# One-hot product and its transposes at a pair's beginning, norm parameters and last norm's rows ahead of the loop of rounds, router subtractions on VectorE

## The chip, the core and the metric

The kernel runs on one core of a Trainium2 chip. The metric is the device time of one execution in microseconds (us). In the profile PE is TensorE's matmuls, PEld its weight loads, DVE is VectorE, ACT is ScalarE, POOL is GpSimd and SP is SyncE, which issues most of the DMAs. L1612 is line 1612 of the kernel before; in the kernel after the same statements stand some lines lower.

## The reference, cut to what matters

Two blocks run one after the other on 256 tokens of width 1024. The first, two hybrid layers, takes the time to about 838 us and is not touched. The second has two layers; each is a mixer (three kinds of attention behind one input projection, and an output projection), a layer norm, a router and a mixture of experts (MoE), and a second layer norm.

```python
def second_block(...):
    h = layer_norm(x, ln_in_g, ln_in_b)
    for l in range(DEPTH):                                    # 2
        mix = mixer_sublayer(h, ...)
        h = layer_norm(DEEPNORM_ALPHA * h + mix, ln1_g[l], ln1_b[l])
        ffn = grouped_moe(h, router_w, router_bias, exp_w_gate[l], exp_w_up[l], exp_w_down[l])
        h = layer_norm(DEEPNORM_ALPHA * h + ffn, ln2_g[l], ln2_b[l])
    return h

def grouped_moe(h, ...):                                      # 16 experts in 4 groups, 2 per token
    scores = sigmoid(h @ router_w)
    ...                                                       # best group, two best experts in it
    dense_gates = ...                                         # gate of each token and expert, mostly 0
    for e in range(N_EXPERTS):
        a = silu(h @ w_gate[e]) * (h @ w_up[e])               # 1024 -> 512
        y = y + dense_gates[:, e:e + 1] * (a @ w_down[e])     # 512 -> 1024
    return y
```

Everything is float32.

## The kernel before

**The stages.** In the second block, layer 0's mixer runs from about 840 to 984 us, its router to 996, its MoE to 1220; then come a branch, a norm and layer 1's mixer to 1366, its router to 1378, its MoE to 1603, and the last norm with the output.

**The MoE.** Experts work on slots: each has 64 slots per round, to which its tokens are gathered by a matmul with a one-hot matrix `oh` (L1546, L1562). A round has all experts; further rounds, in the loop `tc.For_i(1, rounds)` (L1716), are for experts with more than 64 tokens, and with these data the loop's body is passed over. Its branch stops all engines at a barrier. Experts go in eight pairs. `pair` computes the gate projection `pg` and the up projection `pu` (two calls of `proj`, 8 steps of the contraction each, L1597), the activation `a` on VectorE (L1633, L1634), its four transposes on TensorE (L1638), the copy `aT` on ScalarE (L1640), and the down projection from `wd` (L1597 again). The results are scaled by the slot's gate and split in a high and a low part (L1671 on ScalarE, L1672 on VectorE). `combine` brings them back to token order by matmuls with `got` (L1655) and adds them to the state (L1657). `combine` is a generator of two steps, which runs in the next pair: `pump()` calls one step behind the up projection and one behind the copy `aT`.

`combine_T` makes `got` and the slots' gates `gs`: a product of one-hot and gate on VectorE (`go`, L1607), two transposes (L1612), and two VectorE operations on them (L1615, L1616). In pairs 0 to 6 it is called behind the copy `aT`, in front of the down projection. The last pair differs (`done` is set): it calls `combine_T` ahead of the gate projection, pumps the pair before's combine between gate and up, and splits the down projection in four quarters of 256 columns. Within a quarter, behind the first of four steps (`mid` at k == 1), it combines the quarter before and takes its statistics for the norm (L802).

**Weights.** SP issues the transfers in the order of the code, into a ring of 1 MB places; a pair needs 12 of them (4 gate, 4 up, 4 down). A place is filled again when TensorE has read it. Behind the last pair SP issues the first pieces of the next mixer's input projection `w_in`.

**Router.** VectorE ranks the scores in small operations (L1506 to L1530), TensorE turns the mask `mb` into positions, and VectorE makes the one-hot. ScalarE meanwhile normalises the state and copies it to `hn[0]`; `hn[1]` is the rest, by subtraction: columns 0 to 511 on POOL (L1502), the others on VectorE (L1569).

**Norm and mixer's start.** Behind the branch, `norm_params` (L810 to L817) takes mean, reciprocal deviation and their product from the statistics; `normalise` (L826, L827) applies them; 16 transposes (L855) with copies in high and low parts (L1207 to L1210) lead to the first gemm, whose weights are split in two parts by ScalarE (L278) and VectorE (L279). The last norm brings its gain and shift rows to all partitions by four matmuls (L833); VectorE's six operations (L1758, L1759) read them from PSUM, POOL's two (L1750, L1751) from copies in SBUF.

## Time and profile before

| | us |
|---|---|
| median of 3 runs | 1619.72 (1618.51 to 1620.62) |
| the profiled execution | 1618.68 |
| its span in the trace | 1616.4 |
| PE busy in the span | 1510.0 (93%) |
| DVE / ACT / POOL busy | 976.5 / 736.3 / 251.8 |
| bytes moved by DMA | 419.71 MB, mean 260 GB/s |

The span is what the trace covers; 2.3 us of the execution lie around it. A row of a timeline has the start of a group of like instructions, the group's length, engine, line, operation, what is written and read, the count (xN), and in brackets how long the engine had been idle and what ended that. One 512-wide float32 matmul of the program stands there as two records. The page says that TensorE is busy nearly all the time, but the mean hides stages with different limits: in the MoE stages the transfers are saturated as well, and around the branch and in the tail nearly everything waits for short chains on VectorE and ScalarE. Stages have to be read apart.

### The profile page before, as it was taken

How to read it: one execution, taken by the hardware profiler on the slowest of the kernel's cores; microseconds unless marked ns; L12 is line 12 of the kernel's file. 1: busy time of each engine (PE TensorE's matmuls, PEld its weight loads, DVE VectorE, ACT ScalarE, POOL GpSimd, SP SyncE). 2: the span in 40 equal slices, each digit the busy share in tenths (PEclk: the TensorE clock that was granted, in tenths of full speed). 3: DMA queues.
4: the chain of work that ended last, by engine and by line, in shares of the span. 5: the costliest groups of instructions: out<-in, count | busy, mean ns of one | idle time of the engine just before them, and what ended most of it. 6: DMA issues, size and time to landing. Idle time of an engine off the chain costs nothing. (4 is left out here: it accounts for less than half of the span.)

```text
span 1616.4 us, 24413 instructions
## 1 busy us (share of the span) xinstructions
PE 1510.0 (93%) x9211; PEld 1092.7 (68%) x9211; DVE 976.5 (60%) x1894; ACT 736.3 (46%) x1403; POOL 251.8 (16%) x279
## 2 busy tenths in 40 slices
PE   6999999999999999999989998999988998999996
PEld 5877888888887888888878775334437776344332
DVE  4869777777786767777557774322137767222224
ACT  3466645655456664556446664112115565111112
POOL 0334640001242363000003100000001210000000
PEclk9999999999999999999999998999998999999998
DMA  9766769557854675965526368999985558899992
GB/s 346 245 215 236 261 219 353 181 179 235 313 186 136 218 271 185 318 207 174 164 73 209 128 222 300 403 407 407 407 314 168 179 180 315 314 407 406 407 405 92
DMA packets 278476, 419.71 MB, mean 260 GB/s; under 512 B 12722, under 2 KB 147748, under 8 KB 278348
## 3 DMA queue, kind: packets, MB, share of 16 engines
q1 hardware_dynamic: 273052, 398.63, 69.5%
q0 software_dynamic: 5152, 19.14, 3.4%
q8 instruction: 77, 1.26, 0.3%
q14 instruction: 51, 0.42, 0.1%
q10 hardware_dynamic: 144, 0.26, 0.0%
HBM read 416.94 MB, written 1.05 MB: 259 GB/s over the span
## 5 line engine op out<-in xcount | busy, mean ns | idle before, releaser
L279 DVE TENSOR_TENSOR split<-raw,split 128x1024 fp32r<-128x1024 f32 (+4 forms) x330 | 411.7, 1251 | 114.3 <-ACT split L278 111.2
L289 PE MATMUL mm<-hl,split 128*128 128x512 f32 x1168 | 412.6, 397 | 0.0
L278 ACT CAST split<-raw 128x1024 fp32r<-128x1024 f32 (+4 forms) x330 | 328.7, 1000 | 131.6 <-PE mm L323 69.5
L290 PE MATMUL mm<-hl,split 128*128 128x256 f32 x1168 | 326.3, 279 | 1.0 <-DVE split L279 1.0
L289 PEld LDWEIGHTS mm<-hl,split 128*128 128x128 f32 x1168 | 219.0, 187 | 50.4 <-issue 0.7
L1597 PE MATMUL mm<-raw,xg 128*64 128x512 f32 x1024 | 230.9, 602 | 1.1 <-ACT xg L1564 1.1
L290 PEld LDWEIGHTS mm<-hl,split 128*128 128x128 f32 x1168 | 220.3, 189 | 1.5 <-DVE split L279 1.3
L1597 PEld LDWEIGHTS mm<-raw,xg 128*64 128x64 f32 x1024 | 71.5, 138 | 136.5 <-issue 118.7
L289 PE MATMUL mm<-ahl,split 128*128 128x512 f32 x352 | 123.4, 395 | 0.0
L306 ACT COPY t<-mm 128x256 f32<-128x256 f32 x152 | 56.4, 371 | 142.7 <-PE mm L290 133.7
L1597 PE MATMUL mm<-raw,t 128*64 128x512 f32 (+1 forms) x576 | 114.8, 549 | 1.4 <-ACT t L1640 1.4
L321 PE MATMUL mm<-split,hl 128*128 128x512 f32 (+4 forms) x272 | 102.3, 376 | 4.2 <-ACT split L278 3.2
L290 PE MATMUL mm<-ahl,split 128*128 128x256 f32 x352 | 98.3, 279 | 0.3 <-DVE split L279 0.3
L322 PE MATMUL mm<-split,hl 128*128 128x512 f32 (+4 forms) x272 | 96.4, 355 | 1.0 <-DVE split L279 1.0
L323 PE MATMUL mm<-split,hl 128*128 128x512 f32 (+4 forms) x272 | 96.4, 355 | 0.3 <-POOL hl L1210 0.2
L306 DVE TENSOR_TENSOR t<-mm,t 128x256 f32<-128x256 f32 x140 | 59.1, 422 | 47.9 <-ACT t L306 47.7
L1633 DVE SCALAR_TENSOR_TENSOR t<-t,mm 128x512 f32<-128x512 f32 x16 | 11.0, 686 | 123.3 <-ACT t L1632 123.3
L1597 PEld LDWEIGHTS mm<-raw,t 128*64 128x64 f32 x576 | 39.4, 137 | 63.8 <-issue 53.4
L1672 DVE SCALAR_TENSOR_TENSOR t<-mm,s,t 128x512 fp32r<-128x512 f32 (+1 forms) x36 | 24.9, 692 | 94.9 <-ACT t L1671 94.9
L1671 ACT ACTIVATE t<-mm,s 128x512 fp32r<-128x512 f32 (+1 forms) x36 | 23.0, 640 | 129.9 <-PE mm L1597 129.9
L289 PEld LDWEIGHTS mm<-ahl,split 128*128 128x128 f32 x352 | 66.0, 187 | 15.5 <-ACT t L1095 0.2
L1640 ACT COPY t<-at 128x512 f32<-128x512 f32 x16 | 9.4, 586 | 129.7 <-PE at L1638 129.7
(426 smaller groups left out, 2563.3 us busy)
## 6 DMA issues: line engine op xcount, KB each, us to landing
raw<-in_exp_w_gate_dram SPq DMA_DIRECT2D x128, 512.0 KB
raw<-in_exp_w_up_dram SPq DMA_DIRECT2D x128, 512.0 KB
raw<-in_exp_w_down_dram SPq DMA_DIRECT2D x128, 512.0 KB
raw<-in_w_in_dram SPq DMA_DIRECT2D x54, 1024.0 KB
raw<-in_w_ada_dram SPq DMA_DIRECT2D x30, 1024.0 KB
raw<-in_w_gate_dram SPq DMA_DIRECT2D x22, 1024.0 KB
raw<-in_w_up_dram SPq DMA_DIRECT2D x22, 1024.0 KB
ada<-in_w_ada_dram POOLq DMA_DIRECT2D x18, 1024.0 KB, 5.8
```

What stands on the lines that cost most here:

```text
L278: S.copy(h, src)
L279: V.tensor_sub(lo, src, h)
L289: PE.matmul(ps, h[:, k], x[k0 + k], start=first and k == 0, stop=False)
L290: PE.matmul(ps[:, :T], lo[:, k], x[k0 + k][:, :T], start=False, stop=last and k == K - 1)
L306: return S.copy(b[:, :T], ps[:, T:]), V.tensor_add(dst, ps[:, :T], b[:, :T])
L321: PE.matmul(ps[i][:, :n], xh, h[:, j], start=f, stop=False)
L322: PE.matmul(ps[i][:, :n], xh, lo[:, j], start=False, stop=False)
L323: PE.matmul(ps[i][:, :n], xl, h[:, j], start=False, stop=z)
L1597: PE.matmul(ps[64 * b:64 * b + 64, :], lhs(k, b), ws[k][b], start=k == 0, stop=k == nk - 1)
L1633: V.scalar_tensor_tensor(th, th, 1.0, pg, op0=OP.add, op1=OP.mult)
L1671: S.activation(yh[:, sl], pd_[:, :w], AF.Copy, scale=gs)
L1672: V.scalar_tensor_tensor(yl[:, sl], pd_[:, :w], gs, yh[:, sl], op0=OP.mult, op1=OP.subtract)
```

## The change

- `combine_T` becomes a generator. Its product `go` is emitted at the beginning of each pair, its transposes and the rest in the gate projection, at `mid`, which moves from k == 1 to k == 3. The last pair loses its `pump(2)` between gate and up, so that the combine of the pair before runs behind up as in the other pairs. `mid` at k == 3 holds for the quarters of the last pair too.
- The router's two subtractions of POOL go to VectorE.
- `norm_params` is computed ahead of the loop of rounds, into a kept tile `keep` (and again at the end of the loop's body). In layer 0 the first two weight splits of the next mixer come ahead of the loop as well. In layer 1 the last norm's four rows are made there and copied to SBUF (`lnb`, two copies on VectorE, two on ScalarE).
- The last norm reads gain and shift from `lnb`, and subtracts the mean where it added its negative. An ordering of the second weight splits behind the normalising (`held`) is dropped.
- The mixers' start: only the first half of the columns is transposed ahead of the first gemm, the other two quarters as steps within it.

On SP one transfer changes its place: the second `mla_w_uq` of layer 1 goes ahead of two gate pieces.

```diff
@@ mixer
-        transposed(ev)
+        transposed(ev, (0, 1))
+        def rest():
+            for q in (2, 3):
+                transposed(ev, (q,))
+                yield
+        steps.append(rest())
...
-        rq = rank_in(xs_gemm(k_chunks(W, l, KD, 0, 384), hl, 384), 384, cqT, 3, "mla_q")
+        rq = rank_in(xs_gemm(k_chunks(W, l, KD, 0, 384), hl, 384, 1), 384, cqT, 3, "mla_q")
@@ moe, router
-                    if q == 0:
-                        G.tensor_sub(hn[1][:, i, sl], y[:, i, sl], hn[0][:, i, sl])
...
+        V.tensor_sub(hn[1][:, 0, 0:512], y[:, 0, 0:512], hn[0][:, 0, 0:512])
         gained = gains(f"ln1_{l}", [mm_bank(), mm_bank()])
...
         oh = one_hot(0, pos)
+        V.tensor_sub(hn[1][:, 1, 0:512], y[:, 1, 0:512], hn[0][:, 1, 0:512])
@@ moe, pairs
-                if mid and k == 1:
+                if mid and k == 3:
...
+            yield
             pb = at_bank()
...
-            return got, gs[:, 0:1]
+            yield got, gs[:, 0:1]
...
-            if done:
-                got, gs = combine_T(p, oh)
+            turned = combine_T(p, oh)
+            next(turned)
+            box = []
             pg, pu = mm_bank(), mm_bank()
-            proj(pg, xs, wg, KD, more=more)
-            if done:
-                pump(2)
+            proj(pg, xs, wg, KD, lambda: box.extend(next(turned)), more)
+            got, gs = box
...
-            if not done:
-                got, gs = combine_T(p, oh)
@@ ahead of the loop of rounds
+        keep = sml.tile([P, 8], F32, tag="keep", name=nm("keep"), bufs=1)
+        norm_params(keep)
...
         if l + 1 < L:
-            mixer_first(l + 1)
...
+            wf = mixer_first(l + 1)
+            split_early(wf[0][1][:, 0:2])
+            split_early(wf[0][1][:, 2:4])
...
+            lnb = unit(U_LAST, "lnb").rearrange("p (v q n) -> p v q n", v=2, q=2)
+            for q in range(2):
+                for v in range(2):
+                    pb = gain_bank(f"ln2_{l}", v, q)
+                    (S.copy if v else V.tensor_copy)(lnb[:, v, q], pb)
@@ tail
-            V.scalar_tensor_tensor(t, t, mean[:, i:i + 1], g_[q], op0=OP.add, op1=OP.mult)
-            V.scalar_tensor_tensor(t, t, rs[:, i:i + 1], b_[q], op0=OP.mult, op1=OP.add)
+            V.scalar_tensor_tensor(t, t, mean[:, i:i + 1], lnb[:, 0, q], op0=OP.subtract, op1=OP.mult)
+            V.scalar_tensor_tensor(t, t, rs[:, i:i + 1], lnb[:, 1, q], op0=OP.mult, op1=OP.add)
```

**TensorE, pair 1 of layer 0.** Before, the two transposes of `combine_T` (L1612) stand between the second combine step (L1655) and the down projection (L1597 reading the turned activation `t_10473`):

```order
L1638 MATMUL at_10468<-con,t_10456 128x128 x4
L1655 MATMUL at_10475<-t_10381,got_10355 128x512
L1655 MATMUL at_10475<-t_10382,got_10355 128x512
L1655 MATMUL at_10479<-t_10381,got_10355 128x512
L1655 MATMUL at_10479<-t_10382,got_10355 128x512
L1612 MATMUL at_10486<-con,t_10483 128x128 x2
L1597 MATMUL mm_10493<-raw_10409,t_10473 64x512 x4
```

After, from the pair's gate projection to its down projection:

```order
L1604 MATMUL mm_10424<-raw_10385,xg_10191 64x512 x4
L1604 MATMUL mm_10424<-raw_10388,xg_10191 64x512 x2
L1620 MATMUL at_10432<-con,t_10421 128x128 x2
...
L1661 MATMUL at_10485<-t_10381,got_10281 128x512
L1661 MATMUL at_10485<-t_10382,got_10281 128x512
L1661 MATMUL at_10489<-t_10381,got_10281 128x512
L1661 MATMUL at_10489<-t_10382,got_10281 128x512
L1604 MATMUL mm_10493<-raw_10409,t_10483 64x512 x4
```

The transposes (now L1620) have gone into the gate projection, behind three of its eight steps; the down projection follows the combine step directly.

**TensorE, last pair of layer 0.** Before, with transposes ahead of the gate projection, the combine of the pair before between gate and up, and a quarter's combine behind one of four steps of the next quarter (x2 of 8 matmuls):

```order
L1612 MATMUL at_11384<-con,t_11381 128x128 x2
L1597 MATMUL mm_11391<-raw_11354,xg_11162 64x512 x4
L1655 MATMUL at_11409<-t_11328,got_11315 128x512
L1655 MATMUL at_11409<-t_11329,got_11315 128x512
...
L1655 MATMUL at_11421<-t_11342,got_11315 128x512
L1597 MATMUL mm_11392<-raw_11357,xg_11162 64x512 x4
...
L1638 MATMUL at_11446<-con,t_11442 128x128 x4
L1597 MATMUL mm_11455<-raw_11369,t_11451 64x256 x8
L1597 MATMUL mm_11468<-raw_11372,t_11451 64x256 x2
L1655 MATMUL at_11471<-t_11464,got_11387 128x256
```

After:

```order
L1604 MATMUL mm_11384<-raw_11348,xg_11162 64x512 x2
L1620 MATMUL at_11392<-con,t_11381 128x128 x2
L1604 MATMUL mm_11384<-raw_11348,xg_11162 64x512 x2
...
L1604 MATMUL mm_11385<-raw_11366,xg_11162 64x512 x4
L1661 MATMUL at_11430<-t_11328,got_11249 128x512
...
L1661 MATMUL at_11434<-t_11329,got_11249 128x512
L1646 MATMUL at_11438<-con,t_11426 128x128 x4
L1661 MATMUL at_11447<-t_11341,got_11249 128x512
...
L1661 MATMUL at_11451<-t_11342,got_11249 128x512
L1604 MATMUL mm_11455<-raw_11369,t_11443 64x256 x8
L1604 MATMUL mm_11468<-raw_11372,t_11443 64x256 x6
L1661 MATMUL at_11475<-t_11464,got_11395 128x256
```

The combine of the pair before has gone behind up, around the activation's transposes (L1646), and a quarter's combine behind three of four steps (x6 of 8).

**VectorE, router of layer 0.** Before, from the last group comparison to the one-hots (`ing` is L1524, `rank` L1525, `mb` and `mask` L1530):

```order
L1522 TENSOR_REDUCE s_10156<-s_10154 128x2
L1525 TENSOR_REDUCE s_10158<-t_10157 128x32
L1524 TENSOR_TENSOR s_10155<-s_10154,s_10156 128x8
L1530 SCALAR_TENSOR_TENSOR mb_10170<-s_10158,s_10155 128x32
L1530 SCALAR_TENSOR_TENSOR mask_10171<-s_10158,s_10155 128x32
L1541 SCALAR_TENSOR_TENSOR pos_10184<-at_10178,mask_10171 128x32
L1546 TENSOR_TENSOR oh_10186<-pos_10184,con 128x256 x2
L1546 TENSOR_TENSOR oh_10519<-pos_10184,con 128x256 x2
```

After:

```order
L1527 TENSOR_REDUCE s_10154<-s_10152 128x2
L1536 TENSOR_TENSOR hn_10112<-state_8374,hn_10111 128x512
L1529 TENSOR_TENSOR s_10153<-s_10152,s_10154 128x8
L1530 TENSOR_REDUCE s_10156<-t_10155 128x32
L1574 TENSOR_TENSOR hn_10112<-state_8374,hn_10111 128x512
L1535 SCALAR_TENSOR_TENSOR mb_10168<-s_10156,s_10153 128x32
L1535 SCALAR_TENSOR_TENSOR mask_10169<-s_10156,s_10153 128x32
L1547 SCALAR_TENSOR_TENSOR pos_10183<-at_10177,mask_10169 128x32
L1552 TENSOR_TENSOR oh_10185<-pos_10183,con 128x256 x2
L1576 TENSOR_TENSOR hn_10112<-state_8374,hn_10111 128x512 x2
```

Two subtractions `hn` have come in among the ranking operations ahead of `mb`, and the second group's one-hot has left this place.

## Rows read from the trace of the kernel before

**Rows 1.** Busy times of one stretch, MoE of layer 0: engines, clock, DMA share, GB/s.

```profile
1004.00:1204.00 200.00, 190.00 (x908) 76.36 (x904) 51.67 (x98) 30.65 (x53) 0.00 (x0) 1.00 1.05 400
```

**Rows 2.** Waits of PE in the same stretch: us in total, times, longest.

```profile
PE at L1612 <- DVE t L1607: 9.0, 7, 1.8
```

**Rows 3.** Timeline of PE, pair 1: start, us, engine, line, tiles, count, idle.

```profile
1021.29 13.90 PE L1597 MATMUL mm<-raw,xg 128*64 128x512 f32 x64
...
1038.90 0.44 PE L1612 MATMUL at<-con,t 128*128 128x128 f32 x2 [1.20 <-DVE t L1607]
```

**Rows 4.** Timeline of DVE, pair 0's end and pair 1.

```profile
1022.23 0.75 DVE L1672 SCALAR_TENSOR_TENSOR t<-mm,s,t 128x512 fp32r<-128x512 f32 x1 [2.68 <-ACT t L1671]
...
1035.89 2.67 DVE L1657 TENSOR_TENSOR state<-state,at 128x512 f32<-128x512 f32 x4
1038.48 0.48 DVE L1607 TENSOR_TENSOR t<-oh,gate 128x128 f32<-128x128 f32 x2
```

**Rows 5.** Timeline of PE, last pair of layer 0.

```profile
1194.62 2.13 PE L1655 MATMUL at<-t,got 128*128 128x512 f32 x8
...
1204.57 0.66 PE L1638 MATMUL at<-con,t 128*128 128x128 f32 x4 [0.79 <-DVE t L1634]
1205.90 2.38 PE L1597 MATMUL mm<-raw,t 128*64 128x256 f32 x20 [0.68 <-ACT t L1640]
...
1212.64 1.95 PE L1597 MATMUL mm<-raw,t 128*64 128x256 f32 x16
...
1215.80 1.52 PE L1597 MATMUL mm<-raw,t 128*64 128x256 f32 x12
```

**Rows 6.** Busy times near the end of layer 1's transfers.

```profile
1582.00:1584.00 2.00, 2.00 (x12) 0.71 (x10) 0.00 (x0) 0.00 (x0) 0.00 (x0) 1.00 0.39 137
```

**Rows 7.** Timeline of PE, last quarter of layer 1.

```profile
1598.21 1.52 PE L1597 MATMUL mm<-raw,t 128*64 128x256 f32 x12
```

**Rows 8.** Timelines of POOL and of DVE, router of layer 0.

```profile
985.71 2.50 POOL L1502 TENSOR_TENSOR hn<-state,hn 128x512 fp32r<-128x512 f32 x2 [46.25 <-ACT hn L1500]
...
986.07 0.93 DVE L1524 TENSOR_TENSOR s<-s,s 128x8 f32<-128x8 f32 x1
987.03 1.22 DVE L1530 SCALAR_TENSOR_TENSOR mb<-s,s 128x32 bf16<-128x32 f32 x1
988.17 0.18 DVE L1530 SCALAR_TENSOR_TENSOR mask<-s,s 128x32 f32<-128x32 f32 x1
...
990.22 1.28 DVE L1569 TENSOR_TENSOR hn<-state,hn 128x512 fp32r<-128x512 f32 x2
```

**Rows 9.** Timelines of DVE and of PE behind the branch, layer 0 to 1.

```profile
1222.47 0.39 DVE L810 BATCH_NORM_AGGREGATE s<-s 128x2 f32<-128x24 f32 x2 [2.22 <-issue]
...
1228.19 0.96 DVE L279 TENSOR_TENSOR split<-raw,split 128x768 fp32r<-128x768 f32 x1 [0.57 <-ACT split L278]
...
1224.86 3.68 PE L855 MATMUL at<-con,state 128*128 128x128 f32 x16 [5.83 <-ACT state L826]
```

**Rows 10.** Busy times around that branch.

```profile
1220.00:1231.00 11.00, 5.83 (x23) 5.24 (x24) 6.23 (x17) 7.79 (x13) 0.89 (x3) 0.53 0.75 261
```

**Rows 11.** Timeline of all engines, the tail.

```profile
1604.68 0.39 DVE L810 BATCH_NORM_AGGREGATE s<-s 128x2 f32<-128x24 f32 x2 [2.02 <-issue]
...
1608.40 1.41 DVE L1758 SCALAR_TENSOR_TENSOR state<-state,s,at 128x512 f32<-128x512 f32 x2 [2.15 <-ACT t L1748]
...
1609.72 1.40 DVE L1759 SCALAR_TENSOR_TENSOR state<-state,s,at 128x512 f32<-128x512 f32 x2
1610.01 1.27 POOL L1750 TENSOR_TENSOR state<-state,t 128x512 f32<-128x512 f32 x1 [239.32 <-ACT state L1749]
...
1612.65 0.38 ACTq L1761 DMA_DIRECT2D out_dram<-state  x1
```

**Rows 12.** Timelines of POOL and DVE, the first block's gates.

```profile
159.46 2.15 POOL L722 TENSOR_TENSOR acc<-acc,t 128x512 f32<-128x512 f32 x1 [2.21 <-ACT t L720]
...
160.77 1.39 DVE L726 SCALAR_TENSOR_TENSOR gate<-ada,cs,gate 128x512 f32<-128x512 f32 x1
```

More of the change, by code (lines that the diff above doesn't have):

```diff
@@ L174 @@
     RING_MOE = (22, 8, 10, 11, 0, 12, 13, 9, 17, 18, 19, 20, 21, 5, 6, 7, 3, 4)
+    U_LAST = 12
     UNIT = {8: 2560}
@@ L802, in stats, with norm_params @@
             V.bn_stats(bs[0][:, i, 6 * q:6 * q + 6], src[i] if src else st[0][:, i, w * q:w * q + w])
-    last_mv = [None]
-    def norm_params():
-        mv = last_mv[0] = small(4).rearrange("p (a b) -> p a b", a=2)
+    def norm_params(keep=None):
+        mv = (keep[:, 0:4] if keep is not None else small(4)).rearrange("p (a b) -> p a b", a=2)
         for i in range(2):
             V.bn_aggr(mv[:, i], bs[0][:, i])
-        y, h, z, rs, nb = small(2), small(2), small(2), small(2), small(2)
+        y, h, z = small(2), small(2), small(2)
+        rs, nb = (small(2), small(2)) if keep is None else (keep[:, 4:6], keep[:, 6:8])
         S.activation(y, mv[:, :, 1], AF.Abs_reciprocal_sqrt, bias=epst[:, 2:3])
@@ L1710, in moe @@
         rounds = nc.values_load(nri[0:1, 0:1], min_val=1, max_val=4)
+        keep = sml.tile([P, 8], F32, tag="keep", name=nm("keep"), bufs=1)
+        norm_params(keep)
+        splits[:] = U_SPLIT
+        nsplit[0] = 0
         if l + 1 < L:
-            mixer_first(l + 1)
-        loop_ring = tuple(u for u in RING_MOE if l + 1 == L or u not in ring["units"])
+            wf = mixer_first(l + 1)
+            split_early(wf[0][1][:, 0:2])
+            split_early(wf[0][1][:, 2:4])
+            taken = ring["units"] + U_SPLIT[:2]
+        else:
+            lnb = unit(U_LAST, "lnb").rearrange("p (v q n) -> p v q n", v=2, q=2)
[3 more added lines that the diff above has]
+                    (S.copy if v else V.tensor_copy)(lnb[:, v, q], pb)
+            taken = (U_LAST,)
+        loop_ring = tuple(u for u in RING_MOE if u not in taken)
         first_ring = ring["units"]
@@ L1727, in moe @@
                 stats(q, new=False, n=4)
+            norm_params(keep)
         if l + 1 < L:
@@ L1730, in moe @@
             mixer_ahead(l + 1)
+            return keep
+        return keep, lnb
     first = mixer_first(0)
@@ L1736 @@
     for l in range(L):
-        moe(l, mixer(l))
+        keep = moe(l, mixer(l))
         if l + 1 < L:
-            held[:] = 3 * [normalise(*norm_params())]
-    g_, b_ = [[gain_bank(f"ln2_{L - 1}", v, q) for q in range(2)] for v in range(2)]
-    rs, nb = norm_params()
-    mean = small(2)
-    V.tensor_scalar_mul(mean, last_mv[0][:, :, 0], -1.0)
+            normalise(keep[:, 4:6], keep[:, 6:8])
+    keep, lnb = keep
+    mean, rs, nb = keep[:, 0:4:2], keep[:, 4:6], keep[:, 6:8]
     t = st[0][:, 1, 0:512]
-    gb = [t512() for _ in range(2)]
-    for s_, d_ in zip((g_, b_), gb):
-        S.copy(d_, s_[0])
     S.activation(t, t, AF.Identity, bias=nb[:, 1:2], scale=rs[:, 1:2])
-    G.tensor_mul(t, t, gb[0])
-    G.tensor_add(t, t, gb[1])
+    G.tensor_mul(t, t, lnb[:, 0, 0])
+    G.tensor_add(t, t, lnb[:, 1, 0])
     for q in range(2):
```

## The prediction

> **What bounds the kernel now.** I read the page's slices first, then the windows cut at the stages, then the waits of TensorE, and last the timelines where those waits are. In a MoE stage two streams run side by side for 200 us: TensorE is busy 190.0 of 200 us and the DMA engines move 400 GB/s with a share over 1 [rows 1]. Both cannot be the limit, and the end of the stage tells which is: in layer 1 the transfers are down to 137 GB/s between 1582 and 1584 us [rows 6], while the last quarter of the last down-projection ends at 1598.21 + 1.52 = 1599.73 [rows 7]. The bytes end at about 1582 + 2 x 137/400 = 1582.7, so TensorE runs 17.0 us behind them. Within the stage TensorE's own path is the bound, and the bytes are a floor 17 us lower. TensorE's idle time there has nearly one source: seven waits at L1612, 9.0 us in all, longest 1.8 [rows 2]; layer 1 shows the same seven. Six are the 1.20 us in front of a down-projection [rows 3], one, of 9.0 - 6 x 1.20 = 1.8 us, stands ahead of the last pair.
>
> **Pairs 1 to 6.** L1607 (0.48 for two) stands on VectorE behind four L1657 additions [rows 4], so the transposes come 1.20 late. Now the multiply stands right behind the second L1672 of the pair before, and the transposes after three of the eight steps of the gate projection. Is it there in time? The 64 matmuls of gate and up take 13.90 from 1021.29 [rows 3]; the transposes come after 12 of them, at 1021.29 + 12 x 0.217 = 1023.9. L1672 started at 1022.23 with 0.75 [rows 4]; the first product follows about 0.25 behind its end, near 1023.3, the second by 1023.5. The margin is some 0.4 to 0.7, so no wait. The down-projection could then start at 1038.90 - 1.20 = 1037.70, if the turned activation is there; from the four transposes to it the last pair takes 1205.90 - 1204.57 = 1.33 [rows 5], covered by the combine step that takes about as long. The transposes still cost up to 0.44 [rows 3], in the gate projection. Net per pair between 1.20 and 1.57; I take 1.35, so 6 x 1.35 = **8.1** (7.2 to 9.4). Pair 0 has no such wait and stays.
>
> **Pair 7.** The wait of 1.8 goes. The eight combine matmuls between gate and up, 2.13 [rows 5], go behind up, four on each side of the activation's transposes, where 0.79 and 0.68 of idle time lie now [rows 5]. From up's end to the down-projection it was 0.79 + 1.33 = 2.1. The pairs ahead, which have the order that pair 7 gets now, need 1037.70 less 1021.29 + 13.90, which is 2.5 [rows 3]. Sum 1.8 + 2.1 - 0.4 = **3.5**. The down-projection quarters repeat every 1215.80 - 1212.64 = 3.16 us, of which their own matmuls are 1.95 [rows 5]. The other 1.2 is the combine of the quarter before, though one of this width should take a quarter of the 2.13, 0.53: its second matmul waits for L1672. At step 3 in place of step 1 its inputs are there, so a quarter takes about 2.5, over three quarters **2.0** (1.5 to 2.7).
>
> **Router.** L1524 and the first L1530 last 0.93 and 1.22 while POOL's L1502 runs; the second L1530, alike, lasts 0.18 behind it [rows 8]. That is 0.75 + 1.04 = 1.8 us on the path to the gather. Two subtractions on VectorE at 1.28/2 = 0.64 [rows 8] take 1.28 of it back, less overlap: **0.6** earlier per layer (0 to 0.8). The Trainium skill ("SBUF — State Buffer", section "SBUF: two separate sides") calls the port pair of VectorE and GpSimd an exclusive lock for an operation with two SBUF inputs. The 0.93 and 1.22 agree. By shared bandwidth instead, the small operations would hardly have grown and the move would lose some 1 us a layer; the sum does not use the rule.
>
> **Which end is later.** TensorE's path shortens by 0.6 + 8.1 + 3.5 + 2.0 = 14.2 per layer (12.5 to 16). The floor: the last bytes, a notice of 0 to 2.5 us (I take 1.5: the last output transfer, with its bytes, needs under 3.8 from issue to the end of the span, 1616.4 less 1612.65 [rows 11]), then one quarter, 1.95, with 0.53 of combine: 4.0. That leaves 17.0 - 4.0 = 13.0, and 13.4 since the transfers restart some 0.4 earlier behind the router: they wait for gate matmuls that follow the gather. The floor decides: **13.4 per layer** (12.4 to 14.5), layer 0 taken alike, 26.8 in all. TensorE will then wait for expert weights in the last pair, by well under 1 us at a time.
>
> **Boundary between layers.** Ahead of the branch VectorE now does the parameters, about 1.5, and two subtractions of a 768-wide split, 0.96 each [rows 9], which are 3 us more before the barrier (the parameters by the tail, where L810 starts at 1604.68 and VectorE is done with them at 1608.40 - 2.15 = 1606.25 [rows 11]). Its 2.22 of issue [rows 9] stays. Behind it the parameters are gone, so normalising comes about 1.7 us later than now, counted from the last quarter. In return only 8 of 16 transposes (3.68 for 16 [rows 9]) stand ahead of the first gemm, the splits are there, and ScalarE's table load behind the barrier is off the path. First matmul 10.7 in place of 10.9 behind the last quarter; the rest follows a little more slowly as the second half is pumped in: **0.3 lost** (1.5 either way). Mixer 0 has the new order alone, **0.3 gained** (0 to 0.8). The second mla_w_uq transfer that now goes ahead of two gate pieces on SP costs nothing: TensorE is far behind those.
>
> **Tail.** The four row matmuls and the copies move ahead of the branch, under the parameters; the chain before the barrier grows by some 2.4 (parameters 1.4, two copies of about 0.5), and what came behind it (3.7 from L810 to L1758 [rows 11], which now starts at once) goes. So the final operations start 1.1 earlier. But their gain rows are now in SBUF. With one input in PSUM two of them last 1.40 while POOL multiplies in 1.27, no more than the 1.41 of the two before [rows 11]; an operation with SBUF inputs alone lasted 1.39 beside POOL's 2.15 [rows 12], twice its 0.7. If six of 0.70 and POOL's two of 1.27 exclude each other in full they need 6.7 rather than about 4.2, and the gain is gone: **0** (from 1.2 lost to 1.2 gained). The same page of the Trainium skill, its section "Who interferes with whom", says that the later of the two fully blocks; by it the tail loses, without it the tail gains 1.2.
>
> **Sum.** 26.8 - 0.3 + 0.3 + 0 = 26.8. The profiled execution is 1618.68: 1616.4 of span and 2.3 around it, 1.04 under the median. 1618.68 - 26.8 = 1591.9; against the median, **1592.9**.
>
> **Rivals.** (a) *The waits come back in part.* If the multiply is late by more than 0.7, the transposes stop the gate projection; their 0.44 does not overlap; or the up-projection's end is again held by `a`. At 0.75 in place of 1.35 per pair the path gives 0.6 + 4.5 + 3.5 + 2.0 = 10.6 a layer, less than the floor leaves: 21.2 in all, 1598.5. For it: a margin of 0.4 to 0.7 only. Against: VectorE is busy a quarter of the stage [rows 1], and its queue in front of the multiply holds nothing but L1672.
> (b) *The change moves the wait whole.* The multiply still stands behind something that ends late in each pair, and the 8.1 stay: 6.1 a layer, gain 12.2, 1607.5. For it: the queue is strict. Against: the order shows nothing between.
> (c) *The floor lies lower and the ends gain.* The notice is short (14.5 a layer), tail 1.2, boundary 1: gain 31, 1588.5.
> (d) *Slower than before: the clock.* From 1220 to 1231 the granted clock is 0.53 of full speed in the mean, mostly the lower of its two levels (1.2 and 2.4 GHz), after TensorE stood idle 5.83 us [rows 9, 10]. If new small waits for weights in the last pair let the clock fall there, its work takes twice as long: gate and up 13.9, combine 2.1, transposes 0.7, four quarters with their combines 10.0, in all 26.7 more a layer [rows 3, 5]; 2 x 26.7 - 26.8 is 26.6 slower, 1646. It decides from 13.4 us of such work per layer on. Against: over the stage, waits of 1.20 and 1.8 left the clock at 1.00 [rows 1 to 3].
>
> **Chances.** Forecast (1589.5 to 1596) 0.66; (a) and worse ends, 1596 to 1603, 0.17; (c) 0.08; (b) 0.05; no difference 0.02; (d) 0.02. The range takes the forecast, the nearer two thirds of (a), and the nearer half of (c): **1587.5 to 1600**. A measurement of this kernel can tell about 0.2% (3.2 us) from no change. Faster 0.96, within it 0.02, slower 0.02.
>
> **What would show it.** No waits at the combine's transposes; down-projections some 1.5 earlier in each pair; first waits for expert weights in the last pair, and only there; the last quarter ending about 4 us behind the last bytes; L1524's and L1530's successors at 0.2 us. I am wrong if the last quarter ends well over 5 us behind the bytes (then the path gave less), if the gate projection shows a wait at its transposes, or if the clock falls before the branch. In the tail, operations of 1.4 beside POOL show the exclusion, 0.7 its absence.

## The result, and the profile after

The changed kernel takes 1598.55 us (median of 4 runs, 1596.76 to 1603.16) against 1619.12 of the kernel before, measured beside it: a ratio of 0.988, with a 95% interval of 0.985 to 0.991. That is some 20 us faster (15 to 24), where 26.8 were forecast. It lies within the stated range, at its far end.

The profiled execution took 1603.16 us with a span of 1601.4, 15.0 under the span of the kernel before. A part of that lies in the first block, whose instructions the change does not touch: in the 130 us from 700 to 830 the trace of the changed kernel has 741 matmuls, that of the kernel before 753, with the granted clock at 1.00 in both. So stages are compared below from the first block's last transposes (L867) on, which stand at 839.1 us before and at 842.5 after.

| stage, us | before | changed | changed, second profile |
|---|---|---|---|
| first block's last transposes to router 0's position matmuls | 149.2 | 152.4 | 152.3 |
| to the last quarter of layer 0 | 229.0 | 216.9 | 217.6 |
| to router 1's position matmuls | 153.5 | 156.9 | 157.7 |
| to the last quarter of layer 1 | 228.9 | 216.6 | 217.2 |
| to the end of the span | 16.6 | 16.2 | 16.2 |
| sum | 777.3 | 758.9 | 761.0 |

Both MoE stages gained about 12 us, and both mixers lost 3 to 4. (The first and third stage hold a mixer and a router's ranking.) These sums give a gain of 18.4 and 16.3 us, the medians 20.6 and, in the second run, 18.4; a trace shows one execution, and where the other two us lie is not shown.

**The MoE stage.** Same stretch as [rows 1], busy times of the changed kernel, and TensorE's waits from router 1 to the end of layer 1's MoE (us in total, times, longest):

```profile
1004.00:1204.00 200.00, 198.76 (x962) 80.27 (x962) 52.09 (x96) 34.92 (x60) 0.00 (x0) 1.00 1.04 398
```

```profile
PE at L1540 <- DVE mb L1535: 3.2, 1, 3.2
PE at L1568 <- ACT hn L1507: 0.8, 1, 0.8
PE at L1646 <- DVE t L1642: 0.8, 1, 0.8
PE at L1661 <- ACT t L1677: 0.6, 1, 0.6
```

TensorE is busy 198.76 of 200 us (190.0 in [rows 1]). The line of [rows 2] is gone: nothing waits at the combine's transposes, and among the waits of matmuls no line names a transfer of expert weights. The weight loads (PEld) are another matter. In the last pair of layer 1 the 52 matmuls behind the combine's transposes last 12.09 us, in layer 0 11.47, and one weight load among them waits 0.52 for a transfer of the up projection's weights (0.28 to 0.29 lie between its neighbours):

```profile
1561.08 12.09 PE L1604 MATMUL mm<-raw,xg 128*64 128x512 f32 x52
1571.24 0.62 PEld L1604 LDWEIGHTS mm<-raw,xg 128*64 128x64 f32 x5 [0.52 <-DMA raw<-in_exp_w_up_dram]
```

The last pair of layer 0 on TensorE, which answers to [rows 3, 5]:

```profile
1185.24 2.74 PE L1604 MATMUL mm<-raw,xg 128*64 128x512 f32 x12
1187.92 0.44 PE L1620 MATMUL at<-con,t 128*128 128x128 f32 x2
1188.29 11.47 PE L1604 MATMUL mm<-raw,xg 128*64 128x512 f32 x52
...
1201.07 1.17 PE L1661 MATMUL at<-t,got 128*128 128x512 f32 x4
1202.17 3.24 PE L1604 MATMUL mm<-raw,t 128*64 128x256 f32 x28
1205.35 0.73 PE L1661 MATMUL at<-t,got 128*128 128x256 f32 x4
...
1207.89 0.73 PE L1661 MATMUL at<-t,got 128*128 128x256 f32 x4
```

The transposes (1187.92) stand in the gate projection without a wait in brackets, the down projection follows the second combine step at once, and a quarter repeats every 1207.89 - 1205.35 = 2.54 us (3.16 in [rows 5]).

**Transfers at the end of layer 1**, and TensorE's last quarter, which answer to [rows 6, 7]:

```profile
1580.00:1582.00 2.00, 2.00 (x18) 1.19 (x14) 1.27 (x5) 0.47 (x1) 0.00 (x0) 1.00 0.30 100
1582.00:1584.00 2.00, 2.00 (x18) 1.18 (x18) 1.69 (x5) 0.47 (x1) 0.00 (x0) 1.00 0.01 4
```

```profile
1584.55 0.65 PE L1604 MATMUL mm<-raw,t 128*64 128x256 f32 x4
```

The bytes end at about 1580 + 2 x 100/400 = 1580.5, the quarter at 1585.20: 4.7 us behind, where it had been 17.0.

**The mixer's start.** TensorE behind the branch, layer 0 to 1, which answers to [rows 9], and the granted clock (the figure behind POOL's) in that stretch:

```profile
1219.73 0.47 PE L855 MATMUL at<-con,state 128*128 128x128 f32 x1 [6.27 <-ACT state L826]
1220.84 1.75 PE L855 MATMUL at<-con,state 128*128 128x128 f32 x7 [0.64 <-DVE state L827]
1222.40 0.69 PE L322 MATMUL mm<-split,hl 128*128 128x384 f32 x1
...
1225.11 0.69 PE L324 MATMUL mm<-split,hl 128*128 128x384 f32 x1 [0.34 <-POOL hl L1210]
...
1227.52 1.05 PE L855 MATMUL at<-con,state 128*128 128x128 f32 x4
...
1236.40 0.45 PE L324 MATMUL mm<-split,hl 128*128 128x384 f32 x1 [0.92 <-POOL hl L1210]
...
1237.21 0.29 PE L322 MATMUL mm<-split,hl 128*128 128x288 f32 x1
```

```profile
1228.00:1230.00 2.00, 2.00 (x9) 2.00 (x8) 1.38 (x2) 1.15 (x2) 0.00 (x0) 0.50 0.48 184
1230.00:1232.00 2.00, 2.00 (x14) 1.96 (x13) 1.00 (x3) 1.03 (x3) 0.71 (x1) 0.93 0.03 8
```

The last quarter of layer 0 ended at 1211.74. The first gemm starts 10.7 us behind it (1222.40), as before (10.9), but ends only at 1237.21, 25.5 behind it, where it had been 21.6. In it stand the later transposes (1227.52) and two waits for POOL's halves of the activations, 0.34 and 0.92. The clock is at its lower level until 1230.3, 10.5 us behind the first transpose; in the kernel before it was back 6.0 us behind it: the window from 1230 to 1231 has 0.57 there, which puts it at 1230.9 for a first transpose at 1224.86 [rows 9].

**The tail**, which answers to [rows 11], POOL and VectorE:

```profile
1592.17 1.26 POOL L1769 TENSOR_TENSOR state<-state,lnb 128x512 f32<-128x512 f32 x1 [271.99 <-ACT state L1768]
1592.90 2.74 DVE L1777 SCALAR_TENSOR_TENSOR state<-state,keep,lnb 128x512 f32<-128x512 f32 x2 [2.44 <-ACT state L1768]
1593.51 1.59 POOL L1770 TENSOR_TENSOR state<-state,lnb 128x512 f32<-128x512 f32 x1
...
1595.57 1.40 DVE L1778 SCALAR_TENSOR_TENSOR state<-state,keep,lnb 128x512 f32<-128x512 f32 x2
```

VectorE's first two operations need 2.74 us beside POOL's, in place of 1.41.

### The profile page after: what moved, and what is told of

Its sections match the earlier page's. It is cut to its first block, busy times and chain, and to the rows that moved or that the text cites. A ratio compares the mean times of both kernels' runs of the same rounds, so it can differ in the third digit from the quotient of the medians.

```text
span 1601.4 us, 24444 instructions
## 1 busy us (share of the span) xinstructions
PE 1515.9 (95%) x9211; PEld 1096.0 (68%) x9211; DVE 977.1 (61%) x1899; ACT 735.0 (46%) x1401; POOL 246.6 (15%) x275
## 5 line engine op out<-in xcount | busy, mean ns | idle before, releaser
L322 PE MATMUL mm<-split,hl 128*128 128x512 f32 (+4 forms) x272 | 104.1, 383 | 4.5 <-ACT split L279 3.2
L324 PE MATMUL mm<-split,hl 128*128 128x512 f32 (+4 forms) x272 | 98.3, 361 | 2.4 <-POOL hl L1210 2.3
L323 PE MATMUL mm<-split,hl 128*128 128x512 f32 (+4 forms) x272 | 97.4, 358 | 0.5 <-DVE split L280 0.5
L290 PEld LDWEIGHTS mm<-ahl,split 128*128 128x128 f32 x352 | 66.0, 188 | 15.8 <-ACT t L1095 0.2
L291 PEld LDWEIGHTS mm<-ahl,split 128*128 128x128 f32 x352 | 66.4, 189 | 0.6 <-DVE split L280 0.6
```

The lines of the kernel that those rows point to most:

```text
L290: PE.matmul(ps, h[:, k], x[k0 + k], start=first and k == 0, stop=False)
L291: PE.matmul(ps[:, :T], lo[:, k], x[k0 + k][:, :T], start=False, stop=last and k == K - 1)
L322: PE.matmul(ps[i][:, :n], xh, h[:, j], start=f, stop=False)
L323: PE.matmul(ps[i][:, :n], xh, lo[:, j], start=False, stop=False)
L324: PE.matmul(ps[i][:, :n], xl, h[:, j], start=False, stop=z)
```

## The experiments

**The changed kernel again.** No edit.

> The changed kernel itself once more, as the one to compare the others with. Theory A (the new order of transposes at a mixer's start keeps TensorE at the lower clock for longer, about 3 us per layer): the stretch from the last quarter of layer 0 to the second router's position matmuls is 156 to 157 us again (153.5 in the kernel before), and the first gemm of that mixer ends 25 to 25.5 us behind the last quarter (21.6 before). Theory B (the 3.4 us lost there, and what was lost ahead of the first router, is chance of one execution, as in the first block, which the change does not touch): the stretch falls back to about 153.5. The time is 19 to 21 us under the kernel before in either case.

1598.86 us (1596.90 to 1607.10), ratio 0.988 (0.985 to 0.991). The stage to router 1 is 157.7, and the first gemms end 25.1 us behind the last quarter and 19.7 behind the first block's transposes, as in the first profile (25.5 and 19.7; before 21.6 and 17.4). It had 741 matmuls in the stretch from 700 to 830 again. So the loss at the mixers' starts is no chance of one execution, and the pace in the first block did not change either from one profile of this kernel to the next. In the last pair the 52 matmuls took 12.20 us in layer 0 here, with a weight load that waits 0.64 for the up weights, and 11.80 in layer 1.

**The order of transposes undone.**

```diff
-        transposed(ev, (0, 1))
...
-        steps.append(rest())
+        transposed(ev)
...
-        rq = rank_in(xs_gemm(k_chunks(W, l, KD, 0, 384), hl, 384, 1), 384, cqT, 3, "mla_q")
+        rq = rank_in(xs_gemm(k_chunks(W, l, KD, 0, 384), hl, 384), 384, cqT, 3, "mla_q")
```

> The changed kernel with one part undone: all 16 transposes ahead of the first gemm again, nothing pumped within it. Theory A (the transposes' order holds the clock low): 5 to 6 us faster than the changed kernel (24 to 26 under the kernel before), the first gemm of layer 1's mixer ends 21 to 22.5 us behind the last quarter, and the clock is back about 6 us behind the first transpose in place of 10.5. Theory B (the longer chain ahead of the barrier, parameters and two splits, is what costs): no more than 1.5 us faster than the changed kernel, and the stretch stays at 156 us.

1593.80 us (1592.63 to 1594.71), ratio 0.985 (0.982 to 0.988): 5 us faster than the changed kernel. The times alone do not prove the cause, since the first block, the same in both, ended at 838.5 here and at 842.5 and 844.4 in the changed kernel's profiles; the mixers' starts are measured from marks behind it. The mixer's start on TensorE:

```profile
1214.04 0.47 PE L855 MATMUL at<-con,state 128*128 128x128 f32 x1 [6.27 <-ACT state L826]
1215.15 3.46 PE L855 MATMUL at<-con,state 128*128 128x128 f32 x15 [0.65 <-DVE state L827]
1218.27 0.67 PE L322 MATMUL mm<-split,hl 128*128 128x384 f32 x1
```

The last quarter ended at 1206.06. The transposes start 8.0 us behind it, as in the changed kernel; the first gemm starts 1.5 later (12.2) and still ends earlier: 22.6 behind the last quarter, and 17.0 behind the first block in mixer 0 (25.1 to 25.5 and 19.7 in the changed kernel). Theory A holds in size: 2.7 us a mixer. The clock was back 14.9 behind the last quarter (18.5 in the changed kernel), not as early as theory A said, so it explains only part. What remains against 21.6 in the kernel before is theory B's, parameters and splits ahead of the branch. It is small and not well measured: two later runs with the same start of this mixer have 22.6 (`r3_order`) and 21.6 (`r2_tail_psum`), so the loss is between 0 and 1.0 us.

**The one-hot part alone**, on the kernel before: the parts of the diff in `proj`, `combine_T` and `pair`, nothing else.

> The kernel before with the one-hot part alone (product at the pair's beginning, transposes at step 3 of the gate projection, the last pair's combine behind up, quarters combined at step 3). If the parts add up: position matmuls to the last quarter 216.5 us in both layers (229.0 before), so 24 to 25 us under the kernel before, and all mixer stretches as before (153.5). If the transfers are the floor that the prediction took them for, TensorE shows waits for expert weights in the last pair; if its own path is still the later end, there are none and the last quarter ends 4.5 us or more behind the last bytes.

1599.04 us (1595.31 to 1602.80), ratio 0.988 (0.985 to 0.992). From the first block on: 149.0, 216.3, 155.1, 217.3, 16.3, in sum 754.0, which is 23.3 under the kernel before and 5 to 7 under the changed kernel. By the stages the one-hot part is the whole of the gain. The times don't show the 5 to 7 us: the two medians are equal (1599.04 and 1598.86). The longest wait of its matmuls in layer 0's stage:

```profile
PE at L1639 <- DVE t L1635: 0.8, 1, 0.8
```

None is for weights, and the 52 matmuls of the last pair take 11.38, so in layer 0 TensorE's own path is still the later end. In layer 1 they take 12.11, and a weight load waits 0.54 for the up weights: there the transfers have caught up with it. The stage to router 1 was 155.1, not 153.5, though its first gemm ended at 21.5 as before; such differences of one to two us further on in a mixer also stand between two runs of one kernel (153.7 and 155.3 for the order undone, `r1_order` and `r3_order`), and I read nothing from them.

**One-hot part and router.** As the run before, with the router's lines of the diff.

> The kernel before with the one-hot part and the router's subtractions on VectorE, nothing else. If POOL and VectorE excluded each other there, L1524's and L1530's successors take 0.2 us, the position matmuls come 0.5 to 0.7 us earlier behind the mixer, and the time is 1 to 1.5 us under that of the one-hot part alone. If the move only exchanges one load for another, the time is equal to it within 0.5 us. By theory A this kernel is 5 us faster than the changed kernel, by theory B too; the run with the order alone undone tells them apart.

1598.82 us (1593.58 to 1602.86), which cannot be told from the run before. In the trace the ranking on VectorE is shorter:

```profile
990.04 0.68 DVE L1529 TENSOR_TENSOR hn<-state,hn 128x512 fp32r<-128x512 f32 x1
990.63 0.16 DVE L1522 TENSOR_TENSOR s<-s,s 128x8 f32<-128x8 f32 x1
...
990.91 0.68 DVE L1567 TENSOR_TENSOR hn<-state,hn 128x512 fp32r<-128x512 f32 x1
991.51 0.18 DVE L1528 SCALAR_TENSOR_TENSOR mb<-s,s 128x32 bf16<-128x32 f32 x1
```

The small operations take 0.16 and 0.18 us between two subtractions of 0.68, where they had been 0.93 and 1.22 [rows 8]. From L1493 to the position matmuls it is 3.59 us (4.35 with POOL), 0.76 less; so the exchange is a gain of that size at this place, and it is too small for the times.

**The clock held, order kept.** Filler: transposes of a constant into an unused bank, where TensorE idles; no result depends on them.

```diff
+    def spin(n):
+        pb = at_bank()
+        for _ in range(n):
+            for j in range(4):
+                PE.transpose(pb[:, j * P:(j + 1) * P], ident, ident)
...
+            spin(10)
             taken = ring["units"] + U_SPLIT[:2]
...
+    spin(8)
     for l in range(L):
...
             normalise(keep[:, 4:6], keep[:, 6:8])
+            spin(3)
```

> The changed kernel, new order of transposes kept, with idle TensorE time at the mixers' starts filled by transposes of a constant into an unused bank (32 ahead of layer 0's first transposes, 40 ahead of the branch and 12 behind it): extra work, no result. If the lower clock is what the new order costs (theory A), the granted clock stays high or returns earlier, the first gemm takes 10 to 11 us of TensorE time in place of 14.5, it ends 17 us or less behind the first block's last transposes (19.7 in the changed kernel) and 21 to 22 behind layer 0's last quarter (25.1 to 25.5), and the time falls by 4 to 6 us. If the order costs by its own waits and work (POOL's halves, transposes inside the gemm), the time falls by under 2 us.

1601.78 us (1600.90 to 1605.96), ratio 0.989 (0.987 to 0.991): no gain in the time. The two mixers went different ways. In mixer 0 the clock stayed up, and the first gemm ended 17.3 us behind the first block's transposes in place of 19.7. In mixer 1 the first transposes came 14.4 us behind the last quarter in place of 8.0, which the next run explains.

**The clock held, order undone**, and the filler in the routers too.

```diff
         next(gained)
+        spin(8)
         pp = at_bank()
```

> The kernel with all transposes ahead of the gemm (r1_order) and the same filler at the mixers' starts, and 32 filler transposes in each router ahead of the position matmuls. If the clock is kept at the upper level there, gather and the first gate matmuls, which show 2.17 and up to 3.7 us at the lower level, take 1.2 and 1.9, so some 2.5 to 3 us a router and 1.5 to 3 us a mixer start are gained: 5 to 10 us under r1_order, 1584 to 1589. If the short filler does not hold the clock, the time is that of r1_order, within 1 us, or up to 1 us more where the filler stands in the way.

1596.01 us (1594.54 to 1598.93), ratio 0.985 (0.983 to 0.987): the 5 to 10 us did not come. Mixer 0 on TensorE, and the clock in its stretch:

```profile
836.46 3.66 PE L112 MATMUL at<-con 128*128 128x128 f32 x32
839.95 1.91 PE L861 MATMUL at<-con,state 128*128 128x128 f32 x16
841.62 0.42 PE L328 MATMUL mm<-split,hl 128*128 128x384 f32 x1
...
844.03 0.44 PE L330 MATMUL mm<-split,hl 128*128 128x384 f32 x1 [0.84 <-POOL hl L1216]
```

```profile
836.00:840.00 4.00, 4.00 (x38) 4.00 (x38) 3.48 (x11) 1.40 (x3) 0.16 (x2) 1.00 0.50 147
840.00:844.00 4.00, 3.08 (x23) 2.38 (x20) 2.48 (x6) 3.11 (x7) 0.72 (x1) 1.00 0.02 4
```

The filler (3.66 us) joins the transposes, the clock is 1.00, and the first gemm ends 16.0 behind the first block. Against 17.3 with the new order this gives the order's own cost at a clock that is up in both: 1.3 us, for transposes inside the gemm and waits for the activations' parts (the trace does not separate them). The other 1.4 of the 2.7 are the clock. The stages from the position matmuls to the last quarter took 215.8 and 216.0 us (217.5 and 216.1 with the order undone alone). In layer 0 the gather's first eight matmuls and the first eight gate matmuls took 1.41 and 1.94, with 2.17 and 3.68 in the order undone, so the expected 2.5 us were there; but the last pair's 52 matmuls took 12.55 for 11.90, with a weight load that waits 0.99 for the up weights. What TensorE gains here comes up against the transfers. At the branch some 8 us were lost: the stage to router 1 is 162.1 us, with 153.7 for the order undone alone. TensorE there, and ScalarE's first operation behind the branch:

```profile
1200.79 4.56 PE L112 MATMUL at<-con 128*128 128x128 f32 x40
1211.06 2.82 PE L112 MATMUL at<-con 128*128 128x128 f32 x12 [5.71 <-DMA raw<-in_w_in_dram]
```

```profile
1206.27 1.52 ACT L832 ACTIVATE state<-state,keep 128x512 f32<-128x512 f32 x2 [2.71 <-POOL fa L1391]
```

The filler ended at 1205.35. ScalarE went on at 1206.27, but TensorE only at 1211.06, 5.71 behind the filler's end, with nothing of its own to wait for: the filler behind the branch needs no data, and the transfer that the profile names for it is not read there.

**Transposes at step 1.** `mid` back to `k == 1` in the changed kernel.

> The changed kernel with the transposes behind the first step of the gate projection (and the quarters' combine behind the first of four) as in the kernel before. The margin that the prediction worked out for step 3 was 0.4 to 0.7 us; step 1 comes 0.87 us earlier. So TensorE should wait at the transposes for the product in each of seven pairs by 0.1 to 0.5 us, and the quarters should repeat every 3.16 us again in place of 2.54. Position matmuls to last quarter: 219 to 221 us, 3 to 4 more than in the changed kernel. If the margin is larger than worked out, no wait shows at the transposes and only the 1.8 us of the quarters are lost.

1611.92 us in a single execution. Position matmuls to the last quarter: 222.5 and 222.8, 5.6 to 6.2 more than in the changed kernel's first profile, and more than the 219 to 221 expected. TensorE's waits in layer 0:

```profile
PE at L1620 <- DVE t L1614: 3.9, 4, 1.0
```

The product comes 1.0 late in the four pairs without a gather (in the others the gather's matmuls give it time), and the quarters are back at their old pace. The expectation had a slip: two steps are 8 of the matmuls, 1.74 us and not 0.87. So at step 3 the margin is 1.74 - 1.0 = 0.7 us, what the prediction took as its upper end.

**The tail's rows from PSUM.** The order undone, and the last norm's rows made again behind the branch for VectorE.

```diff
+    g_, b_ = [[gain_bank(f"ln2_{L - 1}", v, q) for q in range(2)] for v in range(2)]
...
-            V.scalar_tensor_tensor(t, t, mean[:, i:i + 1], lnb[:, 0, q], op0=OP.subtract, op1=OP.mult)
-            V.scalar_tensor_tensor(t, t, rs[:, i:i + 1], lnb[:, 1, q], op0=OP.mult, op1=OP.add)
+            V.scalar_tensor_tensor(t, t, mean[:, i:i + 1], g_[q], op0=OP.subtract, op1=OP.mult)
+            V.scalar_tensor_tensor(t, t, rs[:, i:i + 1], b_[q], op0=OP.mult, op1=OP.add)
```

> r1_order with the last norm's gain and shift rows made by four matmuls behind the branch again and read from PSUM by VectorE's six operations; POOL keeps two rows copied to SBUF ahead of the branch. If VectorE and POOL exclude each other in the changed kernel's tail (two operations 2.74 us there), the six take 0.70 each, none longer than 0.8, and the stretch from the last quarter to the end of the span is 14.7 to 15.5 us in place of 16.2. If the 2.74 has another source (the first operation waits for ScalarE's result, or for code), the long pair stays and the stretch is 16 us or more. The time is 0.5 to 1.5 us under r1_order, or the same.

1594.24 us (1590.74 to 1600.42), ratio 0.984 (0.981 to 0.987); the tail is 16.0 us. All engines:

```profile
1585.59 2.07 PE L833 MATMUL at<-lnrow,lnsel 64*128 64x512 f32 x4 [5.62 <-issue]
1585.78 1.27 POOL L1765 TENSOR_TENSOR state<-state,lnb 128x512 f32<-128x512 f32 x1
1586.42 1.41 DVE L1772 SCALAR_TENSOR_TENSOR state<-state,keep,at 128x512 f32<-128x512 f32 x2 [3.91 <-PE at L833]
...
1587.74 1.40 DVE L1773 SCALAR_TENSOR_TENSOR state<-state,keep,at 128x512 f32<-128x512 f32 x2
```

The pairs of operations take 1.41 and 1.40, also the first, which runs beside POOL's second (1585.78 to 1587.05): with one input in PSUM there is no exclusion. The 0.5 to 1.5 us did not come, because TensorE began the row matmuls only at 1585.59, again 5.6 us behind its last instruction ahead of the branch (1579.97) and 2.0 behind ScalarE and 1.2 behind POOL.

**TensorE late at the branch, and a version from the parts that paid.** The version `r3_best` keeps the one-hot part, the router and the last norm ahead of the branch; it has the transposes ahead of the gemm, layer 0's parameters and splits behind the branch, `spin(8)` ahead of mixer 0 and in the routers, and no POOL in the tail:

```diff
-    S.activation(t, t, AF.Identity, bias=nb[:, 1:2], scale=rs[:, 1:2])
-    G.tensor_mul(t, t, lnb[:, 0, 0])
-    G.tensor_add(t, t, lnb[:, 1, 0])
...
-            if (q, i) == (0, 1):
-                continue
```

> A version put together from what the runs showed: the one-hot part and the router's subtractions as changed; transposes ahead of the first gemm, norm parameters and weight splits of layer 0 behind the branch as in the kernel before; the last norm's parameters and rows ahead of the branch as changed, but its operations all on VectorE, none on POOL; 32 filler transposes where TensorE idles at the first mixer's start and in each router. From the stages of r1_comb_router and r2_spin: 147 from the first block's last transposes to the position matmuls, 215.8 to the last quarter, 153.5 to 154.5 to the second router less 1, 216.0, and a tail of 14.7 to 15.2 if the eight operations take 0.70 each without POOL beside them (16.2 if the 2.74 was not POOL's doing). Sum 746.5 to 749 (777.3 before, 753.5 for r1_order), so 28 to 31 us under the kernel before, 4.5 to 7 under r1_order.

1592.83 us (1588.19 to 1595.00), ratio 0.9825 (0.981 to 0.984): faster than the kernel before by 27 us, and by the ratios some 9 us faster than the changed kernel (0.988; 7 to 9 by the stages behind the first block). Stages 148.5, 215.6, 156.4, 215.4, 16.1, in sum 752.0, where 746.5 to 749 were expected. The two filled places and the first gemms are as expected (16.0 and 21.5); the first stage is 1.5 us and the stage to router 1 some 2 us longer than expected with nothing at their starts to show for it, and the tail did not shorten. In both last pairs a weight load waits 0.8 us for the up weights. The tail's operations on VectorE:

```profile
1582.68 1.41 DVE L1769 SCALAR_TENSOR_TENSOR state<-state,keep,lnb 128x512 f32<-128x512 f32 x2 [2.44 <-issue]
1584.02 1.41 DVE L1770 SCALAR_TENSOR_TENSOR state<-state,keep,lnb 128x512 f32<-128x512 f32 x2
```

With both inputs in SBUF and POOL silent they take 0.70 each, so the 2.74 was POOL's doing; but eight of them take 5.6 us, and VectorE starts 2.44 us behind its parameters, so the end is where it was.

`r3_order`, the order undone once more beside it:

> r1_order again, to stand beside r3_best on the same chip. 24 to 26 us under the kernel before; the stages within 1 us of its first run: 150.0, 217.5, 153.7, 216.1, 16.2.

1595.74 us (1592.94 to 1599.15), ratio 0.984 (0.983 to 0.986); 150.1, 217.6, 155.3, 217.9, 16.2. The stages in sum are 757.0, 3.5 more than in the first profile of the same kernel, though within 1 us in each stage was expected: a difference of that size between two profiles says nothing. In the times it is 3 us behind `r3_best`, with intervals that overlap, so that `r3_best` is the faster one is not shown.

`r3_late` is `r3_best` with `spin(5)` ahead of the branch of layer 0.

> r3_best with 20 more filler transposes (2.3 us) ahead of the branch between the layers, so that TensorE comes to the branch later than without them, though not later than VectorE. If TensorE needs a fixed 5.5 to 5.7 us from its last instruction ahead of the branch to its first behind it (as in the tail before, in r2_tail_psum's and in r2_spin's), the first transposes come 1.7 + 2.3 + 5.6 = 9.6 us behind the last quarter in place of 7.5, although VectorE and ScalarE are ready at 7.5. If the barrier alone holds TensorE (it waits for VectorE, which comes last either way), they stay at 7.5.

1595.10 us in a single execution. TensorE, and ScalarE's normalising, whose first half is done about 0.8 us behind its start:

```profile
1205.22 2.38 PE L112 MATMUL at<-con 128*128 128x128 f32 x20
1212.76 3.50 PE L861 MATMUL at<-con,state 128*128 128x128 f32 x16 [5.16 <-DMA raw<-in_w_in_dram]
```

```profile
1210.31 1.52 ACT L832 ACTIVATE state<-state,s,s 128x512 f32<-128x512 f32 x2 [0.81 <-DVE s L823]
```

The last quarter ended at 1203.58, the filler at 1207.60. The normalised half was there at about 1211.1, TensorE went on at 1212.76: 5.16 us behind its last instruction, 9.2 behind the last quarter (9.6 forecast, 7.5 without filler). So it is TensorE's own way over the branch that holds it, not the barrier alone. The expectation had TensorE reach the branch ahead of VectorE; it came 1.1 us behind VectorE's last instruction (1206.51), and ScalarE's normalising still started 6.7 us behind the last quarter, as in `r3_best`. In the kernel before and in the changed one this time lay just under the wait for the normalised state (5.83 and 6.27 idle) and showed as that.

## Right and wrong, by the steps of the prediction

- **What bounds the stage** (TensorE's path, seven waits): right. The waits are gone and TensorE has 198.76 of 200 us.
- **Pairs 1 to 6**, 1.35 each: the mechanism is right and the size was 0.2 too large. Down projections moved by 1.11 to 1.16 from one pair to the next in layer 1, 6.8 in all for 8.1, and by 1.01 to 1.13 in layer 0; the transposes cost their full 0.37 in the gate projection, and no part of them overlapped. The margin of 0.4 to 0.7 was right (0.7).
- **Pair 7**, 3.5: 3.8 in layer 0, 3.1 in layer 1, where the wait for the up weights took 0.6. **Quarters**, 2.0: 1.84 and 1.86.
- **Router**, 0.6: 0.76 in the ranking.
- **Which end is later**: half right. I had the path 14.2 us shorter and the transfers' floor deciding at 13.4, with waits for weights in the last pair. Behind the position matmuls the stages became 12.1 and 12.4 us shorter. In layer 0 no weight load of the last pair waits beyond the usual 0.3 (11.47 for the 52 matmuls; in the second profile one waits 0.64), so there the path decides, and the term that was mis-sized is the six pairs. In layer 1 the floor is reached: weight loads wait for the up weights, 0.52 the longest, and cost 0.6. The last quarter ends 4.7 us behind the last bytes where the floor was put at 4.0, and 4.7 to 4.9 behind in five profiles of four kernels (`after`, `r1_again`, `r1_comb`, `r2_spin`, `r3_best`) with stages from 215.4 to 217.3 long: what binds is the up weights, not the last down weights that I had counted from. The notice of 1.5 us in that sum was not measured by itself.
- **Boundary and mixer 0**, 0.3 lost and 0.3 gained: this is the step that failed. The first matmul came at 10.7 as worked out, but "the rest follows a little more slowly" was 3.5 to 3.9 us at the end of the first gemm in mixer 1 and 2.3 in mixer 0 against the kernel before, of which the order alone is 2.5 to 2.9 and 2.7. I had counted the transposes' order as a gain because TensorE starts earlier. It starts earlier into the lower clock, with gaps, and the clock comes back later; the order's own waits take the rest. With this one part undone the time fell by 5. The parameters and splits ahead of the branch bought nothing and cost up to 1.0: TensorE's first transpose came 8.0 us behind the last quarter, 7.5 before. Its last instruction ahead of the branch ends 1.7 behind the quarter, and with 5.2 to 5.7 over the branch whatever VectorE has ready, even a chain of no length behind it could have brought the transpose to 6.9 or 7.4 only.
- **Tail**, 0 with an exclusion of VectorE and POOL: 0.4 gained. 2.74 beside POOL, 1.41 with POOL silent, 1.41 beside POOL with a PSUM input show the exclusion. The Trainium skill ("SBUF — State Buffer", section "Who interferes with whom") calls the shared port pair an exclusive lock, so that the second operation waits in full; 2.74 for two, from 1592.90 to 1595.64, with POOL at work until 1595.10, agrees: the second of the two ends 0.54 behind POOL.
- **Sum**: 26.8 forecast; the two MoE stages gave 23.2 to 24.5 in the two profiles, the mixers and routers took 6.6 to 7.3, the tail gave 0.4. None of the rivals was this one; (a), which had the right time (1598.5), had it for another reason. That the time lies within the range is in part luck: the range reached that far for waits that come back in the pairs, and what came was a loss at the mixers' starts, which had been put at nothing.

## What to carry to other kernels

A wait that shows in every repetition on the engine that bounds a stage is worth its length times its count, if the moved work costs the same where it goes: here 1.20 of wait gave 1.13, six times per layer, and the moved transposes cost their 0.37 as before. When such an engine's path has been cut down to the transfers, look at the waits of its weight loads as well as of its matmuls. Work that starts TensorE earlier but in pieces, behind a long idle stretch, is not a gain until the clock is counted: here a gemm that started 1.5 us earlier ended 2.5 to 2.9 later. And before a chain behind a branch is shortened, see when each engine comes back over the branch by itself.

## What was not expected of the hardware

- **TensorE's way over a branch.** From its last instruction ahead of the loop's branch to its first behind it: 5.16 (`r3_late`), 5.6 (`r2_tail_psum`, where no weights are loaded) and 5.71 us (`r2_spin`), while VectorE and ScalarE go on 0.5 to 2.7 us behind VectorE's last. It counts from TensorE's own arrival: with 4.56 us of filler ahead of the branch it was back 11.9 us behind the last quarter, without filler 7.5 to 8.0, while ScalarE's start did not move with the filler. The Trainium skill ("Runtime: NRT & Kernel Launch", section "Instruction fetch mechanics") says that a taken branch out of the fetched window costs a fetch; that would fit, and no run here shows that it is the cause.
- **Two paces at one granted clock.** The first block's same instructions run at 741 or at 752 to 755 matmuls in the 130 us from 700 to 830, both with 1.00 granted. The changed kernel's and the order undone's:

```profile
700.00:830.00 130.00, 130.00 (x741) 112.88 (x740) 88.65 (x126) 69.83 (x112) 4.44 (x6) 1.00 0.49 161
```

```profile
700.00:830.00 130.00, 130.00 (x754) 113.92 (x754) 88.62 (x125) 70.88 (x113) 4.43 (x6) 1.00 0.50 164
```

Twelve matmuls are some 2 us, and the first block ended between 836.3 and 844.4 in the thirteen profiles, which is as much as several parts of this change. The two kernels that were profiled twice kept their pace (741 and 741 for the changed one, 754 and 752 for the order undone), so it may go with the program as well as with the execution; two kernels' times can differ by it. Its cause stays open.
